# The passage from output projection to FFN with VectorE alone, on kept fp32 tiles of the first token half

## The chip, the cores and the metric

The kernel runs on one core of a Trainium2 chip, as one launch. The metric is the device time of that launch in microseconds (us). The five engines run side by side, each taking its own instructions in order: PE (TensorE, matmuls; PEld is its weight load), DVE (VectorE), ACT (ScalarE), POOL (GpSimd) and SP (SyncE, which issues most DMAs).

## The reference, cut to what matters

Two layers of a bidirectional encoder trunk over 1024 tokens of width 1024. The change lies between the end of token mixing and the start of channel mixing, so this is the part that matters:

```python
x = x + gt1 * (y @ w_out[l])                       # output projection
h = rms_norm(x, g_ffn[l]) * (1 + sc2) + sh2        # adaLN norm
f = (silu(h @ w_ffn_gate[l]) * (h @ w_ffn_up[l])) @ w_ffn_down[l]   # D_FF = 2816
x = x + gt2 * f
```

## The kernel before, in words

Activations stand transposed in SBUF: 8 channel tiles of 128 partitions by 1024 tokens, in two token halves A (first 512) and B (last 512). Every operand of a matmul is split into a rounded high part and a low part ("hi", "lo"), and each product is three matmuls (hi hi, hi lo, lo hi). ACT makes the high part, DVE or POOL subtracts it from the fp32 value for the low part.

The gate and up products of the FFN are computed by a Strassen-like scheme with seven products per block f of 128 hidden channels (22 blocks), p = 1 to 7, of 12 matmuls each. The seven data operands (`opnd`) are: operands 0 and 1, the normed half A, channel tiles 0 to 3 and 4 to 7 (called h(0..3,A), h(4..7,A)); and operands 2 to 6, sums and differences of the tiles of both halves. `prep` (L1198) makes operands 2 to 6 in five loops over k = 0 to 3:

- operand 2 = h(k,B) - h(k,A); operand 3 = h(4+k,B) - operand 2; operand 4 = h(4+k,B) - h(k,B);
- operand 5 = h(4+k,B); operand 6 = h(4+k,A) - operand 3.

`w_out` (L1157) runs the last jobs of the output projection. It first does the jobs of half A (`self.run(4)`), then weaves the norm of half A (`norm`, L389, with `h_tile`, L374, for each of 8 tiles) into the jobs of half B, and hands `prep` on as a generator. `add_x` (L1117) adds a finished projection tile to x, out of PSUM, and `square` (L345) then accumulates its square for the norm. `rstd_end` (L357) sums the squares over the partitions by 1-column matmuls and spreads the result by one more matmul.

`ffn` (L1471) starts with eight early jobs, p = 1 and 2 of the first `FIRST` = 4 blocks, which need operands 0 and 1 only; the pieces of `prep` are woven in between by the list `nb_f`. Then come p = 5, 6, 7, 3, 4 of block 0, which take operands 2, 3, 4, 5, 6 in this order, then those of block 1, and so on. The weights of a job are prepared by `load` in `p_job` (L1254): for p = 5, 6, 7, 3 a combination of raw weight tiles (`comb`, L1266), then hi on ACT and lo (L1293) on DVE or POOL. A job's weights are prepared up to three jobs ahead. The raw weights of block f + 1 are loaded by SP when the lo part of p = 4 of block f has been taken. After p = 4 of a block the hidden tile is finished on DVE and ACT (`after`, L1301; tile ffa_A), and the down product of that block follows.

The order on PE is written out by the program. For the other engines here a planner places the instructions by its own costs: an engine takes the instruction that stands earliest in the program among those that the planner holds to be ready. Which engine does an elementwise step is written in the table `TUNE` (L92): 0 is DVE, 1 is POOL. `prep`, `lo_f`, `s_f`, `sq_w` and `ht_w` are the lists that matter: the operations of `prep`; the low parts of the late jobs' weights; the weight combinations; the squares in `w_out`; and the kind of `h_tile` (kind 0 takes one scaled product on DVE, hi on ACT, lo on DVE; kind 1 takes a second ACT pass and lo on POOL).

All elementwise steps of one helper have that helper's line in the profile: L191 is a matmul, L199 an ACT step, L202 a DVE TENSOR_TENSOR, L205 a DVE SCALAR_TENSOR_TENSOR, L352 the sum of squares, L385 the lo of `h_tile` on POOL, L1211 the operations of `prep`.

Of the kernel before, what the change touches and what calls it, by code (L numbers as in the profile page):

```python
# [9 lines left out]
F32 = mybir.dt.float32  # L10
F32R = mybir.dt.float32r
AF = mybir.ActivationFunctionType
ALU = mybir.AluOpType
# [4 lines left out]
HALF = 512  # L18
# [7 lines left out]
U = 1024  # L26
# [34 lines left out]
for l in range(2):  # L61
# [8 lines left out]
               split=[38, 35, 37, 39, 41, 43, 54],  # L70
               lo=[0, 0, 0, 0, 0, 0, 0, 0, 0, 0, 0, 0, 0, 0, 0, 1, 0, 0, 0, 0, 0, 0, 0, 0, 0, 0, 0, 0, 0, 0, 0, 0, 0, 0, 0, 0, 0, 0, 0, 0, 0, 0, 0, 0, 0, 0, 0, 0, 0, 0, 0, 0, 0, 0, 0, 0, 0, 0, 0, 0, 0, 0, 0, 0, 1, 0, 0, 0, 0, 0, 0, 1],
               hi=[0, 1, 1, 1, 1, 0, 0, 0, 0, 0, 0, 1, 0, 1, 0],
# [3 lines left out]
FIRST = 4  # L76
# [6 lines left out]
               split=[35, 39, 36, 36, 43, 43, 55],  # L83
               lo=[0, 0, 0, 0, 0, 0, 0, 0, 0, 0, 0, 0, 0, 0, 0, 1, 0, 0, 0, 0, 0, 0, 0, 0, 0, 0, 0, 0, 0, 0, 0, 0, 0, 0, 1, 0, 0, 0, 0, 0, 0, 0, 0, 0, 0, 0, 0, 1, 0, 1, 0, 0, 0, 0, 1, 0, 0, 0, 0, 1, 0, 0, 0, 0, 1, 0, 0, 1, 0, 0, 0, 1],
               hi=[0, 1, 1, 1, 1, 0, 0, 0, 1, 1, 0, 1, 0, 1, 1],
# [5 lines left out]
T_BIAS[1] = 6  # L91
TUNE = dict(  # L92
    na_w=[3, 14], nb_f=[3, 8] + list(range(9, 15)) + list(range(16, 30)), na_f=[5, 11], nb_m=[3, 8],
    prep=[0, 0, 0, 0, 1, 0, 0, 1] * 2 + [0, 0, 1] * 4 + [0, 1] * 4 + [1, 0] * 2 + [0, 1, 0] * 4,
    ht_w=[0, 1] * 4, ht_a=[0, 1] * 4, ht_b=[0, 1] * 4,
    sq_w=[0, 1] * 8, sq_f=[0, 1] * 8,
    lo_e=[0] * 8, lo_f=[1, 0, 0, 1, 0] * FIRST, s_f=[1] * 4 * FIRST,
    pairs=[[2, 3, 4, 4, 5, 6, 6, 7] for _ in range(FIRST)], post=[0] * FIRST,
    fin=[[8, 15], [26, 31]], fk=[[1] * 8, [0, 1] * 4, [0, 1] * 4], sq_t=[[0, 1] * 4, [0, 1] * 4, [0] * 8],
)  # L100
# [9 lines left out]
NS = ((0, 512), (512, 512))  # L110
# [22 lines left out]
class Trunk:  # L133
# [18 lines left out]
        self.ready = set()  # L152
        self.queue, self.look, self.sq = deque(), 1, {}

# [1 line left out]
    def open(self, name, **tiles):  # L156
        cm = self.tc.tile_pool(name=name, bufs=1)
        pool = cm.__enter__()
        for nm, (n, dt) in tiles.items():
            setattr(self, nm, pool.tile([P, n], dt, name=f"{name}_{nm}"))  # L160
        return cm
# [24 lines left out]
        o = (8 * lo + k) * U + n[0]  # L186
        return self.RA[:, o:o + n[1]]

# [1 line left out]
    def mm(self, out, lhsT, rhs, start, stop):  # L190
        self.nc.tensor.matmul(out=out, lhsT=lhsT, rhs=rhs, start=start, stop=stop)  # L191

# [22 lines left out]
            self.act(hi, src, AF.Copy)  # L215
        self.tt(lo, src, hi.bitcast(F32), ALU.subtract)

# [1 line left out]
    def w_load(self, src, n, hi_eng=0):  # L219
        def go():  # L220
            raw, o = self.f(self.WR(), n), self.WH()
            self.at = o
            hi, lo = self.RA[:, o:o + n], self.RA[:, o + self.WS:o + self.WS + n]
            self.nc.sync.dma_start(out=raw, in_=src)
            self.split(raw, hi, lo, hi_eng)
            return hi, lo
        return go
# [25 lines left out]
        for _ in range(njobs):  # L253
            yield from self.pull()

# [1 line left out]
    def setup(self):  # L257
        nc = self.nc
        self.vec = self.const(2 * V_N + 8)
        self.ident = self.const(P)  # L260
        self.ones = self.const(P)
        self.mod = [self.const(48) for _ in range(DEPTH)]
        self.coef = [self.const(16) for _ in range(DEPTH)]
        self.lam8 = [self.const(12) for _ in range(DEPTH)]
        self.tiny = self.const(36)
        self.st = Ring(self.const(4) for _ in range(12))
        nc.scalar.dma_start(out=self.f(self.T0 + 3 * U, U, 0, 1), in_=self.I["c"])
        nc.scalar.dma_start(out=self.f(self.vec, 2 * V_N + 8), in_=self.I["vecs"])
        nc.scalar.dma_start(out=self.f(self.ident, P), in_=self.I["ident"])
        nc.vector.memset(self.f(self.ones, P), 1.0)  # L270
        self.epsc = self.const(1)
        self.st16 = self.const(16)
        self.nc.vector.tensor_copy(out=self.RA[:, 20 * U:20 * U + P], in_=self.f(self.ident, P))
        nc.vector.memset(self.f(self.epsc, 1), EPS)
        row = self.f(self.T0 + 3 * U, U, 0, 1)
        self.act(row, row, AF.Silu)
        for i in range(2):
            self.mm(self.bank(i), self.f(self.ones, P, 0, 1), row[:, i * HALF:(i + 1) * HALF], True, True)
# [55 lines left out]
        while self.steps is not None:  # L334
            self.bg(1)

# [1 line left out]
    def sumsq(self, n, k, acc, s, eng):  # L338
        if k == 0:
            self.act(acc, self.x(k, n), AF.Square)  # L340
# [49 lines left out]
    def norm(self, l, which, n, bank, ts, kinds):  # L390
        accs = self.sq.pop(n)[0]
        yield from self.rstd_end(n, accs, bank)
        for k in range(8):
            self.h_tile(l, which, n, k, ts[k % 2], accs[0], kinds[k])
        yield

    def h_act(self, l, which, n, k, t, twice=True):
        hi, lo = self.h(k, n, 0), self.h(k, n, 1)
# [15 lines left out]
                evac(b)  # L414
            yield

# [1 line left out]
    def jobs(self):  # L418
        for l in range(DEPTH):
            yield from self.mix_jobs(l)  # L420
# [50 lines left out]
        self.act(self.y(j, *n), b, AF.Copy)  # L471
        self.ready.add((j, n[0]))

# [1 line left out]
    def start(self):  # L475
        nc, l = self.nc, 0
        A, B = NS
# [348 lines left out]
    def k_evac(self, t, n, b):  # L826
        self.act(self.f(self.SK + n[0], n[1]), b, AF.Copy)

# [1 line left out]
    def slot_ones(self):  # L830
        for e in range(2):
            self.nc.vector.tensor_copy(out=self.slot(e, 3, 0, U, 64, 68).rearrange("p (a b) -> p a b", a=8),
# [273 lines left out]
        self.attention(l, fill)  # L1106
        return early

# [1 line left out]
    def y_split(self, j):  # L1110
        for c in (0, HALF):
            self.split(self.y(j, c, HALF), self.RA[:, j * U + c:j * U + c + HALF],
# [43 lines left out]
    def w_out(self, l):  # L1156
        A, B = NS  # L1157
        self.ps_all.i = 2
        self.y_split(7)
        self.x_load(l, 7)  # L1160
        self.c_spread()
        self.warm_sqrt(self.f(self.M0, 1))
        self.raws = Ring([self.f(self.M0 + U, U)])
        self.steps = self.mod_steps([(l, 5)] if l == 0 else [])
        self.bgn = 3
        self.hp = self.open(f"hx{l}", HX=(12 * U, F32R))
        self.pp = self.open(f"prep{l}", FP=(4 * U, F32))
        fp = lambda i: self.FP[:, i * HALF:(i + 1) * HALF]
        t = [self.f(self.T0 + HALF * i, HALF) for i in range(4)]
        self.sq[A] = [t[0], fp(7)], [fp(4), fp(5)], TUNE["sq_w"][:8]  # L1170
        self.run(4)
        na = self.norm(l, 1, A, self.ps_all(), t[2:], TUNE["ht_w"])
        self.sq[B] = [t[1], fp(6)], [fp(4), fp(5)], TUNE["sq_w"][8:]
        self.weave(3, na, TUNE["na_w"])
        self.look = 2
        o = self.WH.items[self.WH.i % 2]
        self.PR = Ring([o, o + U, 34 * U - o, 35 * U - o])
        self.weave(1, na, ())
        self.look = 3
        self.bg_all()  # L1180
        self.bgn = 0
        return self.prep(l, 0)
# [3 lines left out]
        self.nc.sync.dma_start(out=cb, in_=self.I["c"].broadcast_to((P, U)))  # L1186
        self.act(cb, cb, AF.Silu)

# [1 line left out]
    def opnd(self, j, k, lo):  # L1190
        if j in (0, 1):
            return self.h(4 * j + k, NS[0], lo)
# [3 lines left out]
        return self.HX[:, o:o + HALF]  # L1196

    def prep(self, l, bank):  # L1198
        nc, n = self.nc, NS[1]
        accs = self.sq.pop(n)[0]  # L1200
        yield from self.rstd_end(n, accs, bank)
        acc = accs[0]
        fp = lambda i: self.FP[:, i * HALF:(i + 1) * HALF]
        q1 = [fp(k) for k in range(4)]
        t = [fp(4 + k) for k in range(4)]
        q2 = [self.f(self.T0 + HALF * i, HALF) for i in (2, 3)] + \
            [self.f(10 * U + HALF * i, HALF) for i in range(2)]
        turn = iter(TUNE["prep"])

        def tt(out, a, b, op):  # L1210
            (nc.gpsimd if next(turn) else nc.vector).tensor_tensor(out=out, in0=a, in1=b, op=op)  # L1211

        def norm(q, k):
            tt(q, self.x(k, n), acc, ALU.mult)
            self.act(q, q, AF.Identity, scale=self.f(self.coef[l] + 8 + k, 1), bias=self.f(self.mod[l] + 24 + k, 1))

        def parts(j, k, src):
            hi, lo = self.opnd(j, k, 0), self.opnd(j, k, 1)
            self.act(hi, src, AF.Copy)
            tt(lo, src, hi.bitcast(F32), ALU.subtract)  # L1220

        old = lambda j, k, lo: self.opnd(j, k, lo).bitcast(F32)
        for k in range(4):
            norm(q1[k], k)
            tt(t[k], q1[k], old(0, k, 0), ALU.subtract)
            tt(t[k], t[k], old(0, k, 1), ALU.subtract)
            parts(2, k, t[k])
            yield
        for k in range(4):
            norm(q2[k], 4 + k)  # L1230
            tt(t[k], q2[k], t[k], ALU.subtract)
            parts(3, k, t[k])
            yield
        for k in range(4):
            tt(q1[k], q2[k], q1[k], ALU.subtract)
            parts(4, k, q1[k])
            yield
        for k in range(4):
            parts(5, k, q2[k])
            yield  # L1240
        for k in range(4):
            tt(t[k], old(1, k, 0), t[k], ALU.subtract)
            tt(t[k], t[k], old(1, k, 1), ALU.add)
            parts(6, k, t[k])
            yield

# [418 lines left out]
```

## Time and profile before

| | |
|---|---|
| median of 3 runs | 2447.42 us (2445.95 to 2452.44) |
| profiled execution | span 2447.3 us; the page gives no other time for it |
| busy share of the span | PE 92%, PEld 73%, DVE 78%, ACT 41%, POOL 37% |
| chain of work that ended last | PE 65%, DVE 21%, issue 5%, ACT 4%, POOL 2%, DMA 2% |
| granted TensorE clock, mean | 0.963 |

The span is one execution by the hardware profiler. The shares are means over stages of quite different kinds; the passage stands twice in the trace, once per layer, near 485 to 590 us and 1678 to 1781 us. Times are counted from the start of the span. A group "x38" is 38 instructions of one kind in a row. Bracketed behind an instruction is the time its engine sat idle before it, and what ended that.

### The profile page before, as it was taken

How to read it: one execution, taken by the hardware profiler on the slowest of the kernel's cores; microseconds unless marked ns; L12 is line 12 of the kernel's file. 1: busy time of each engine (PE TensorE's matmuls, PEld its weight loads, DVE VectorE, ACT ScalarE, POOL GpSimd, SP SyncE). 2: the span in 40 equal slices, each digit the busy share in tenths (PEclk: the TensorE clock that was granted, in tenths of full speed). 3: DMA queues.
4: the chain of work that ended last, by engine and by line, in shares of the span. 5: the costliest groups of instructions: out<-in, count | busy, mean ns of one | idle time of the engine just before them, and what ended most of it. 6: DMA issues, size and time to landing. Idle time of an engine off the chain costs nothing.

```text
span 2447.3 us, 27382 instructions
## 1 busy us (share of the span) xinstructions
PE 2252.3 (92%) x9754; PEld 1790.4 (73%) x9754; DVE 1920.1 (78%) x2732; ACT 995.3 (41%) x1638; POOL 902.7 (37%) x646
## 2 busy tenths in 40 slices
PE   6987998977999999999989899898799999999996
PEld 4765876765777777778867687677567888888885
DVE  8887789788888888887765676986987777777775
ACT  4375575453222222222354746654422222222234
POOL 4133375255233333333231316642622333333333
PEclk9998999988999999999989999999899999999998
DMA  7323422411233333331221132312111111111111
GB/s 286 104 67 116 132 96 86 148 44 65 67 110 106 110 111 109 108 104 52 78 103 51 50 103 70 120 63 87 36 65 52 52 52 52 52 52 52 52 48 69
DMA packets 77998, 206.94 MB, mean 85 GB/s; under 512 B 8995, under 2 KB 13091, under 8 KB 77862
## 3 DMA queue, kind: packets, MB, share of 16 engines
q1 hardware_dynamic: 74116, 186.55, 23.3%
q10 hardware_dynamic: 3746, 18.66, 2.2%
q8 instruction: 76, 1.25, 0.2%
q14 instruction: 60, 0.49, 0.1%
HBM read 196.79 MB, written 8.39 MB: 84 GB/s over the span
## 4 chain that ended last, share of the span: by engine, by line
PE 65%; DVE 21%; issue 5%; ACT 4%; POOL 2%; DMA 2%; SPq 0%; POOLq 0%; DVEq 0%; ACTq 0%
PE psum L191 65%; DVE plain L202 3%; DVE rounded L202 3%; DVE plain L205 2%; DVE prep_FP L1211 1%; DVE rounded L1293 1%; DMA plain<-in_ada 1%; DVE ffa_A L202 1%; DVE psum L880 1%; DVE plain L313 1%; DVE psum L202 1%; ACT lru_LF L199 1%; ACT plain L199 1%; ACT ffa_A L199 1%; ACT rounded L199 1%
## 5 line engine op out<-in xcount | busy, mean ns | idle before, releaser
L191 PE MATMUL psum<-rounded 128*128 128x512 f32 (+1 forms) x4380 | 1091.0, 398 | 73.4 <-DVE rounded L1293 21.1
L191 PEld LDWEIGHTS psum<-rounded 128*128 128x128 f32 x4380 | 834.2, 193 | 264.2 <-DVE rounded L1293 25.1
L205 DVE SCALAR_TENSOR_TENSOR plain<-psum,plain 128x1024 f32<-128x1024 f32 (+2 forms) x464 | 483.6, 1051 | 200.6 <-PE psum L191 198.4
L199 ACT ACTIVATE rounded<-plain 128x512 fp32r<-128x512 f32 (+4 forms) x464 | 307.0, 668 | 768.9 <-PE psum L191 667.4
L191 PE MATMUL psum<-ffa_A,ffa_DW 128*128 128x512 f32 (+1 forms) x2040 | 531.1, 394 | 19.1 <-ACT ffa_A L199 7.8
L191 PEld LDWEIGHTS psum<-ffa_A,ffa_DW 128*128 128x128 f32 x2040 | 378.0, 189 | 123.0 <-DVE ffa_A L202 14.9
L1266 POOL TENSOR_TENSOR plain<-plain 128x512 f32<-128x512 f32 x176 | 254.2, 1444 | 516.4 <-DMA plain<-in_wu 340.8
L191 PE MATMUL psum<-hx_HX,rounded 128*128 128x512 f32 x1584 | 408.0, 395 | 7.5 <-DVE rounded L1293 4.2
L191 PEld LDWEIGHTS psum<-hx_HX,rounded 128*128 128x128 f32 x1584 | 299.5, 189 | 77.0 <-DVE rounded L1293 5.3
L1293 POOL TENSOR_TENSOR rounded<-plain,rounded 128x512 fp32r<-128x512 f32 x124 | 175.0, 1411 | 324.1 <-ACT rounded L199 324.1
L202 DVE TENSOR_TENSOR plain<-psum,plain 128x512 f32<-128x512 f32 x316 | 211.5, 685 | 31.7 <-PE psum L191 26.2
L202 DVE TENSOR_TENSOR rounded<-plain,rounded 128x512 fp32r<-128x512 f32 (+4 forms) x139 | 150.3, 1092 | 62.1 <-ACT rounded L199 60.9
L917 POOL TENSOR_TENSOR rounded<-qk_PE,rounded 128x512 fp32r<-128x512 f32 (+3 forms) x132 | 140.9, 1074 | 127.0 <-ACT rounded L199 102.4
L199 ACT ACTIVATE plain<-plain 128x512 f32<-128x512 f32 (+4 forms) x205 | 130.5, 644 | 97.8 <-DVE plain L202 58.2
L1293 DVE TENSOR_TENSOR rounded<-plain,rounded 128x512 fp32r<-128x512 f32 x184 | 139.4, 758 | 12.6 <-ACT rounded L199 12.4
L202 DVE TENSOR_TENSOR plain<-plain 128x512 f32<-128x512 f32 (+4 forms) x162 | 142.8, 883 | 6.9 <-ACT plain L199 1.9
L191 PE MATMUL psum<-rounded,v_V 128*65 128x512 f32 (+4 forms) x528 | 128.8, 358 | 14.5 <-ACT rounded L199 4.8
L191 PE MATMUL psum<-qk_QT 128*128 128x512 f32 (+8 forms) x432 | 108.0, 349 | 21.3 <-DVE plain L880 15.3
L199 ACT ACTIVATE ffa_DW<-plain 128x512 fp32r<-128x512 f32 x84 | 53.0, 630 | 155.5 <-PE psum L191 153.9
L202 DVE TENSOR_TENSOR psum<-psum,plain 128x256 f32<-128x256 f32 x240 | 97.7, 410 | 21.0 <-PE psum L191 14.3
L191 PEld LDWEIGHTS psum<-rounded,v_V 128*65 128x65 f32 (+1 forms) x528 | 74.0, 149 | 53.0 <-POOL rounded L917 6.3
L199 ACT ACTIVATE qk_PE<-psum 128x512 f32<-128x512 f32 (+4 forms) x168 | 83.3, 503 | 55.4 <-DVE psum L202 51.3
(124 smaller groups left out, 2031.4 us busy)
## 6 DMA issues: line engine op xcount, KB each, us to landing
plain<-in_ada SPq DMA_DIRECT2D x96, 256.0 KB, 2.5
plain<-in_wg SPq DMA_DIRECT2D x44, 512.0 KB, 3.5
plain<-in_wu SPq DMA_DIRECT2D x44, 512.0 KB, 3.5
plain<-in_wd SPq DMA_DIRECT2D x88, 256.0 KB, 2.6
plain<-in_ada SPq DMA_DIRECT2D x30, 512.0 KB, 3.5
start_AT<-in_ada SPq DMA_DIRECT2D x18, 512.0 KB, 5.7
plain<-in_bias_t ACTq DMA_DIRECT2D x12, 768.0 KB, 4.8
plain<-in_bias_s ACTq DMA_DIRECT2D x12, 736.0 KB, 4.4
```

Of the source, the lines that this page charges most:

```text
L191: self.nc.tensor.matmul(out=out, lhsT=lhsT, rhs=rhs, start=start, stop=stop)
L199: self.nc.scalar.activation(out=out, in_=in_, func=func, **kw)
L202: self.nc.vector.tensor_tensor(out=out, in0=a, in1=b, op=op)
L205: self.nc.vector.scalar_tensor_tensor(out=out, in0=a, scalar=s, in1=b, op0=op0, op1=op1)
L313: self.nc.vector.tensor_tensor_reduce(out=raw, in0=raw, in1=self.f(self.M0, U), op0=ALU.mult, op1=ALU.add, scale=1.0, scalar=0.0, accum_ou ...
L880: self.nc.vector.tensor_tensor_reduce(out=s, in0=s, in1=self.f(bo, a * w).rearrange("p (a b) -> p a b", a=a), op0=ALU.add, op1=ALU.max, sc ...
L917: (self.nc.vector if PLAN[self.l]["lo"][self.step] else self.nc.gpsimd).tensor_tensor(out=pl, in0=p, in1=ph.bitcast(F32), op=ALU.subtract)
L1211: (nc.gpsimd if next(turn) else nc.vector).tensor_tensor(out=out, in0=a, in1=b, op=op)
L1266: comb = lambda out, a, b, op=ALU.subtract: (nc.gpsimd if pool_s else nc.vector).tensor_tensor(out=out, in0=a, in1=b, op=op)
L1293: (nc.gpsimd if pool_lo else nc.vector).tensor_tensor(out=lo, in0=src, in1=hi.bitcast(F32), op=ALU.subtract)
```

## The change

- `TUNE["prep"]` goes; every operation of `prep` is on DVE. In `sq_w`, `ht_w`, `s_f` of block 0 and `lo_f` of block 0 all ones become zeros: squares in `w_out`, lo parts of the A tiles, the four combinations and two lo parts of block 0 go from POOL to DVE.
- The eight scaled A tiles (x times scale times 1/rms, before the shift) stay in fp32 in the upper half of the tile FP, which grows from 4U to 8U columns; `h_tile` no longer alternates two temporaries.
- `prep` works on scaled tiles without shift. In operand 2 the shift cancels. In operands 3, 5 and 6 it enters as the scalar of a SCALAR_TENSOR_TENSOR, in operand 4 as the difference of two shifts (`ds`, one small instruction). The two subtractions of the hi and lo parts of half A become one with the kept tile; the ACT pass that applied scale and shift goes.
- `dynamic_dma_scratch_size=512` is passed when the program is built, which leaves more SBUF for tiles.

```diff
-    prep=[0, 0, 0, 0, 1, 0, 0, 1] * 2 + [0, 0, 1] * 4 + [0, 1] * 4 + [1, 0] * 2 + [0, 1, 0] * 4,
-    ht_w=[0, 1] * 4, ht_a=[0, 1] * 4, ht_b=[0, 1] * 4,
-    sq_w=[0, 1] * 8, sq_f=[0, 1] * 8,
-    lo_e=[0] * 8, lo_f=[1, 0, 0, 1, 0] * FIRST, s_f=[1] * 4 * FIRST,
+    ht_w=[0] * 8, ht_a=[0, 1] * 4, ht_b=[0, 1] * 4,
+    sq_w=[0] * 16, sq_f=[0, 1] * 8,
+    lo_e=[0] * 8, lo_f=[0] * 5 + [1, 0, 0, 1, 0] * (FIRST - 1), s_f=[0] * 4 + [1] * 4 * (FIRST - 1),
...
-            self.h_tile(l, which, n, k, ts[k % 2], accs[0], kinds[k])
+            self.h_tile(l, which, n, k, ts[k % len(ts)], accs[0], kinds[k])
...
+    def kept(self, k):
+        return self.FP[:, (8 + k) * HALF:(9 + k) * HALF]
...
-        self.pp = self.open(f"prep{l}", FP=(4 * U, F32))
+        self.pp = self.open(f"prep{l}", FP=(8 * U, F32))
...
-        na = self.norm(l, 1, A, self.ps_all(), t[2:], TUNE["ht_w"])
+        na = self.norm(l, 1, A, self.ps_all(), [self.kept(k) for k in range(8)], TUNE["ht_w"])
...
-        def norm(q, k):
-            tt(q, self.x(k, n), acc, ALU.mult)
-            self.act(q, q, AF.Identity, scale=self.f(self.coef[l] + 8 + k, 1), bias=self.f(self.mod[l] + 24 + k, 1))
+        ds = self.f(self.st16, 4)
+        self.tt(ds, self.f(self.mod[l] + 28, 4), self.f(self.mod[l] + 24, 4), ALU.subtract)
+
+        def scaled(q, k):
+            self.stt(q, self.x(k, n), sc(k), acc, ALU.mult, ALU.mult)
...
         for k in range(4):
-            norm(q1[k], k)
-            tt(t[k], q1[k], old(0, k, 0), ALU.subtract)
-            tt(t[k], t[k], old(0, k, 1), ALU.subtract)
+            scaled(q1[k], k)
+            self.tt(t[k], q1[k], self.kept(k), ALU.subtract)
             parts(2, k, t[k])
             yield
         for k in range(4):
-            norm(q2[k], 4 + k)
-            tt(t[k], q2[k], t[k], ALU.subtract)
+            scaled(q2[k], 4 + k)
+            self.stt(t[k], q2[k], sh(4 + k), t[k], ALU.add, ALU.subtract)
             parts(3, k, t[k])
             yield
         for k in range(4):
-            tt(q1[k], q2[k], q1[k], ALU.subtract)
+            self.stt(q1[k], q2[k], ds[:, k:k + 1], q1[k], ALU.add, ALU.subtract)
             parts(4, k, q1[k])
             yield
         for k in range(4):
-            parts(5, k, q2[k])
+            hi, lo = self.opnd(5, k, 0), self.opnd(5, k, 1)
+            self.act(hi, q2[k], AF.Identity, bias=sh(4 + k))
+            self.stt(lo, q2[k], sh(4 + k), hi.bitcast(F32), ALU.add, ALU.subtract)
             yield
         for k in range(4):
-            tt(t[k], old(1, k, 0), t[k], ALU.subtract)
-            tt(t[k], t[k], old(1, k, 1), ALU.add)
+            self.stt(t[k], self.kept(4 + k), sh(4 + k), t[k], ALU.add, ALU.subtract)
             parts(6, k, t[k])
             yield
...
-    nc = _bacc.Bacc("TRN2", target_bir_lowering=False, num_devices=1)
+    nc = _bacc.Bacc("TRN2", target_bir_lowering=False, num_devices=1, dynamic_dma_scratch_size=512)
```

## Rows read from the trace of the kernel before

**Rows 1.** Busy time by stretch: window; its length, then busy us (count) per engine, PEclk.
```profile
500.00:525.96 25.96, 20.04 (x84) 15.72 (x83) 21.62 (x27) 14.62 (x25) 12.70 (x8) 0.87 0.14 47
525.96:571.70 45.74, 29.00 (x101) 21.71 (x100) 45.74 (x39) 22.75 (x37) 35.63 (x22) 0.81 0.08 29
571.70:588.20 16.50, 11.62 (x47) 8.16 (x46) 13.79 (x18) 8.34 (x13) 9.82 (x7) 1.00 0.28 83
1692.70:1718.74 26.04, 19.97 (x83) 15.97 (x82) 17.66 (x25) 13.82 (x22) 10.69 (x7) 0.87 0.13 48
1718.74:1764.50 45.76, 29.25 (x98) 21.62 (x97) 45.76 (x39) 22.76 (x37) 35.65 (x22) 0.80 0.07 23
1764.50:1781.15 16.65, 12.96 (x50) 9.40 (x48) 13.95 (x18) 8.43 (x13) 9.83 (x7) 0.91 0.27 81
```

**Rows 2.** Timeline of PE, first layer: start, us, engine, line, operation [idle before <-releaser].
```profile
498.45 9.42 PE L191 MATMUL psum<-rounded 128*128 128x512 f32 x39
512.75 5.11 PE L191 MATMUL psum<-rounded 128*128 128x512 f32 x12 [4.89 <-ACT rounded L199]
...
545.66 4.64 PE L191 MATMUL psum<-rounded 128*128 128x512 f32 x10 [4.33 <-DVE rounded L1293]
...
562.62 4.63 PE L191 MATMUL psum<-rounded 128*128 128x512 f32 x10 [4.77 <-DVE rounded L1293]
...
575.13 2.92 PE L191 MATMUL psum<-rounded 128*128 128x512 f32 x12
...
579.70 2.57 PE L191 MATMUL psum<-hx_HX,rounded 128*128 128x512 f32 x10 [1.18 <-POOL rounded L1293]
...
588.20 1.84 PE L191 MATMUL psum<-ffa_A,ffa_DW 128*128 128x512 f32 x5 [1.72 <-DVE ffa_A L202]
```

**Rows 3.** Timeline of DVE, first layer.
```profile
501.05 1.77 DVE L205 SCALAR_TENSOR_TENSOR plain<-plain 128x512 f32<-128x512 f32 x1
...
503.92 0.74 DVE L205 SCALAR_TENSOR_TENSOR plain<-plain 128x512 f32<-128x512 f32 x1
504.58 0.73 DVE L205 SCALAR_TENSOR_TENSOR plain<-psum,plain 128x512 f32<-128x512 f32 x1
505.24 1.12 DVE L205 SCALAR_TENSOR_TENSOR rounded<-plain,rounded 128x512 fp32r<-128x512 f32 x1
...
529.97 4.79 DVE L1211 TENSOR_TENSOR prep_FP<-prep_FP,rounded 128x512 f32<-128x512 f32 x6
...
571.04 0.68 DVE L1293 TENSOR_TENSOR rounded<-plain,rounded 128x512 fp32r<-128x512 f32 x1
571.64 0.68 DVE L202 TENSOR_TENSOR plain<-psum,plain 128x512 f32<-128x512 f32 x1
573.58 0.69 DVE L1211 TENSOR_TENSOR rounded<-prep_FP,rounded 128x512 fp32r<-128x512 f32 x1 [1.26 <-ACT rounded L199]
```

**Rows 4.** Timeline of POOL, first layer.
```profile
532.60 1.61 POOL L1211 TENSOR_TENSOR hx_HX<-prep_FP,hx_HX 128x512 fp32r<-128x512 f32 x1 [3.10 <-ACT hx_HX L199]
...
575.39 3.02 POOL L1266 TENSOR_TENSOR plain<-plain 128x512 f32<-128x512 f32 x2 [2.51 <-DMA plain<-in_wu]
578.38 1.27 POOL L1293 TENSOR_TENSOR rounded<-plain,rounded 128x512 fp32r<-128x512 f32 x1
```

**Rows 5.** Timeline of PE, second layer.
```profile
1690.91 9.42 PE L191 MATMUL psum<-rounded 128*128 128x512 f32 x39
1706.40 5.46 PE L191 MATMUL psum<-rounded 128*128 128x512 f32 x12 [6.07 <-DVE plain L205]
...
1769.52 2.93 PE L191 MATMUL psum<-rounded 128*128 128x512 f32 x12
...
1781.15 2.50 PE L191 MATMUL psum<-ffa_A,ffa_DW 128*128 128x512 f32 x5 [1.72 <-DVE ffa_A L202]
```

**Rows 6.** DMA queues of the page: queue, kind, packets, MB, share.
```profile
q10 hardware_dynamic: 3746, 18.66, 2.2%
q8 instruction: 76, 1.25, 0.2%
```

More of the change, by code (lines that the diff above doesn't have):

```diff
@@ L1198, in prep @@
     def prep(self, l, bank):
-        nc, n = self.nc, NS[1]
+        n = NS[1]
         accs = self.sq.pop(n)[0]
@@ L1207, in prep @@
             [self.f(10 * U + HALF * i, HALF) for i in range(2)]
-        turn = iter(TUNE["prep"])
-        def tt(out, a, b, op):
-            (nc.gpsimd if next(turn) else nc.vector).tensor_tensor(out=out, in0=a, in1=b, op=op)
-        def norm(q, k):
-            tt(q, self.x(k, n), acc, ALU.mult)
-            self.act(q, q, AF.Identity, scale=self.f(self.coef[l] + 8 + k, 1), bias=self.f(self.mod[l] + 24 + k, 1))
+        sc = lambda k: self.f(self.coef[l] + 8 + k, 1)
+        sh = lambda k: self.f(self.mod[l] + 24 + k, 1)
+        ds = self.f(self.st16, 4)
+        self.tt(ds, self.f(self.mod[l] + 28, 4), self.f(self.mod[l] + 24, 4), ALU.subtract)
+        def scaled(q, k):
+            self.stt(q, self.x(k, n), sc(k), acc, ALU.mult, ALU.mult)
         def parts(j, k, src):
@@ L1219, in parts @@
             self.act(hi, src, AF.Copy)
-            tt(lo, src, hi.bitcast(F32), ALU.subtract)
-        old = lambda j, k, lo: self.opnd(j, k, lo).bitcast(F32)
+            self.tt(lo, src, hi.bitcast(F32), ALU.subtract)
         for k in range(4):
-            norm(q1[k], k)
-            tt(t[k], q1[k], old(0, k, 0), ALU.subtract)
-            tt(t[k], t[k], old(0, k, 1), ALU.subtract)
+            scaled(q1[k], k)
+            self.tt(t[k], q1[k], self.kept(k), ALU.subtract)
             parts(2, k, t[k])
```

## The prediction, on record before the changed kernel ran

> **What bounds the kernel now.** I read the page first: PE is busy nearly throughout, but its row of slices dips twice, at the passage of each layer. Then I cut the two passages into stretches [rows 1]. From 525.96 to 571.70 us DVE is busy for all of 45.74 us while PE runs only 101 matmuls; the second layer repeats this to 0.02 us. Then the timelines of PE and DVE show who ends PE's idle time: mostly the low parts of weights (L1293) or an `add_x` (L205) queued on DVE [rows 2, 3, 5]. So between the start of `prep` and the last weight of block 0 the passage is as long as DVE's queue.
>
> DVE's steps have two lengths there. Where POOL is idle, a TENSOR_TENSOR starts 0.60 us after the one before (571.04, 571.64) and a SCALAR_TENSOR_TENSOR 0.66 us after it (503.92, 504.58, 505.24) [rows 3]. Of the six from 529.97, which take 4.79 us, five at 0.60 leave one of about 1.7: POOL was idle for 3.10 us before its instruction at 532.60 [rows 4]. The 38 steps from 525.96 to 571.64 take 45.7 us, 1.20 each; at 0.60 they would take 22.8. The excess is 22.9 us, and POOL ran 22 instructions in that stretch [rows 1]: each costs DVE 1.04 us.
>
> The Trainium skill (SBUF — State Buffer, "Who interferes with whom") says that of a VectorE instruction with two SBUF inputs and a GpSimd instruction that reads SBUF, the one that comes second blocks until the first is through. By it a POOL instruction would cost DVE its whole length, 1.27 us when alone [rows 4], and the stretch would be 22.8 + 22 x 1.27 = 50.7 us; the trace has 45.7, so the block is a little less than whole. Its bearing here is on the chance of the third rival only, which it lowers.
>
> **The change, part by part.** The sum goes against the profiled execution: the page gives its span, 2447.3 us, and nothing around it; the median of the runs lies 0.1 us above.
>
> *Prep stretch.* Before, DVE did 34 of `prep`'s 52 operations per layer and POOL 18, by the list. After, DVE does 44: scaled 8, shift forms 4 + 4 + 4 + 4 (loops 2 to 5) make 24 SCALAR_TENSOR_TENSOR, and 20 TENSOR_TENSOR are left. At the unblocked steps [rows 3]: 24 x 0.66 + 20 x 0.60 = 27.8 us. The low parts of seven weights stand in the same stretch (two of block 3's early jobs, five of block 0; two of these were POOL's): 7 x 0.60 = 4.2. Of the four combinations of block 0, two need only raw weights and can go into gaps ahead of `prep`; two wait for the buffer of another and stay: 1.2. `ds` is bounded by 0 and one step, 0.6; I take 0.6. One pause for ACT's high part, as the 1.26 at 573.58 [rows 3]. Sum 35.1 us against 45.7: 10.6 us less per layer. Bounds: all four combinations inside and three pauses, 38.8 us; none and no pause, 32.0.
>
> ACT loses 8 passes of `prep` and 4 of `h_tile`; it was busy 22.75 of 45.74 us [rows 1], so this counts nothing, and there is room if a high part comes late.
>
> *Norm of half A.* Four low parts of tiles (0.66 each) and two or three squares (0.60) move to DVE, 2.6 + 1.5 = 4.1 us, against eight POOL instructions that blocked it in 25.96 us [rows 1]. With eight buffers nothing holds the 16 tile steps back, and they stand in the program ahead of the last two `add_x`. The last `add_x` frees the PSUM bank of the first early job: PE ended its 39 projection matmuls at 507.87 and restarted at 512.75; in the second layer 1700.33 and 1706.40 [rows 2, 5]. If the planner keeps program order, 16 x 0.66 = 10.6 us from the first tile step at 501.05 [rows 3], two weights and two `add_x` (2.5) give 514, 1.3 us later than now; counted from 1692.7, 1705.8, 0.6 earlier. If it serves `add_x` as soon as its matmuls end, PE restarts 4.1 and 5.4 us earlier. I take nothing, as nearest the first; both ends go into the range.
>
> *Behind the stretch.* After the last weight PE had 6.3 us until p = 4 ended (571.70 to 578.05) and 7.95 in the second layer [rows 1, 2, 5], since jobs had piled up. After, PE is the follower: two jobs of 2.92 us [rows 2] from about 0.8 us before the last weight, 5.0 us. That gives 1.3 and 2.9 us more. From the end of p = 4 to the first down product 10.15 us pass, 8.7 in the second layer [rows 2, 5]: block 1's weights are still on POOL and DVE finishes the hidden tile, so this I leave. What is late next is block 1's p = 5: its raw weights are loaded by SP only after the last weight of block 0, then two combinations and a low part on POOL; 571.70 to 579.70, 8.0 us [rows 2, 4]. That is 3.0 us after p = 4 in the new order, and its 18 matmuls (4.4 us) then end before the first down product can start. So it costs nothing while the 10 us stay; without them it would hold the gain at 10.6.
>
> *The rest.* Early squares of half A on DVE: one 0.60 step in place of a POOL step ahead of the norm's matmuls; 1.27 - 0.60 = 0.7 us either way [rows 3, 4], taken as 0. The larger FP is opened where attention's tiles ended long before and closed as before: 0. The scratch size: the page's four queues are two of each kind [rows 6], none that POOL feeds, so 0; a longer landing time of SP's loads would show otherwise.
>
> Sum: layer one 10.6 + 1.3 = 11.9, layer two 10.6 + 2.9 = 13.5, together 25.4. PE is near full after each passage, so the shift carries to the end. 2447.3 - 25.4 = 2421.9, against the median **2422 us**. Own range 2414 to 2430.
>
> **Rivals.**
> 1. *The norm stage shortens too.* The planner serves the last `add_x` in time: 4.1 + 5.4 = 9.5 us more, 2412. With the shorter pause the first early job may run at the upper clock level (2.92 instead of 5.1 us for 12 matmuls [rows 2]; it now runs at half rate after 4.89 us idle): 4.4 more, 2408. I set 2410. For it: POOL's locks fill the norm stretch. Against: sixteen tile steps ahead in the program.
> 2. *Block 0's weights queue behind all of `prep`.* Its low parts stand late in the program. Then PE gets p = 5 after 27.8 + 0.6 + 1.2 + 1.3 + 0.6 = 31.5 us, the first job at half rate 5.1, four at 2.9: 48.2 us from the start of `prep` to the end of p = 4, against 52.1 and 53.7: 9.4 us in all, **2438**. For it: L1293 is what PE waits for already at 545.66 and 562.62 [rows 2].
> 3. *The long steps are not POOL's doing but the passage's* (PE, ACT and DMA reading SBUF at the same time). Then 53 DVE steps at 1.20 us take 63.8 us against 45.7: +36 in all, **2484**, slower. It decides at 45.7 / 53 = 0.86 us per step. For it: DVE is already busy for the whole stretch, and the change gives it work. Against: the 0.60 steps of the same kind of instruction with POOL idle. The Trainium skill (Perfetto Trace Analysis, "Optimizing Scalar/DVE Operations") says that work of a saturated DVE may be offloaded to Scalar or even GPSIMD, the reverse of this change; by it one would end on this side. The same paragraph adds that between those two the shared port may leave no gain, and the two step lengths here bear that out.
> 4. *No change.* What is gained is given back: the planner orders the rest of the program otherwise, or block 1 waits for its loads and its hidden tile 10 us longer. About 2446. Against: POOL's and DVE's work behind 571.70 is untouched.
>
> **How the numbers follow.** Forecast 0.46, first rival 0.22, second 0.20, fourth 0.07, third 0.05. About 0.3% (7 us) is what a measurement here can tell from no change. Forecast and first two rivals are faster: 0.88; same 0.07; slower 0.05. The range leaves out the third and fourth and the outer edges of the rest: 2405 to 2439.
>
> **What would show it.** Right: in the prep stretch POOL near 0 instructions, DVE full with steps of 0.60 to 0.66, the stretch 32 to 39 us long; the first early job near 513 and 1706; p = 4 of block 0 ends about 12 us earlier, the first down product too. Wrong: many DVE steps over 1 us without POOL (third); the first early job near 509 (first); PE waiting on L1293 for p = 5 to 4 with the operands long done (second); or a prep stretch that is shorter while the first down product hasn't moved (fourth).

## The result, and the profile after

The changed kernel takes 2417.43 us (median of 4 runs, 2413.6 to 2419.18) against 2448.8 us before (4 runs): ratio 0.9867, 95% interval 0.9851 to 0.9882, 31.4 us faster. The forecast was 2422, its range 2405 to 2439. A second series beside other kernels gave 2415.94 against 2448.58, ratio 0.9864 (0.985 to 0.9877). The profiled execution has a span of 2411.8 us and took 2413.6 us in all, so 1.8 us lie around the span; it is the fastest of its series.

The busy time by stretch of the changed kernel, cut at the same events as [rows 1] (columns as there: window; length, busy us and count of PE, PEld, DVE, ACT and POOL, then PEclk, the granted TensorE clock as a share of full speed, the DMA share and GB/s). Helpers stand one line earlier in this kernel: L190 is a matmul, L198 an ACT step, L201 a TENSOR_TENSOR, L204 a SCALAR_TENSOR_TENSOR; the operations of `prep` now go through the last two.

```profile
500.00:524.96 24.96, 16.45 (x72) 13.09 (x71) 18.74 (x31) 10.54 (x17) 0.00 (x0) 0.86 0.13 42
524.96:558.41 33.45, 27.71 (x105) 20.27 (x103) 33.45 (x54) 18.79 (x31) 0.00 (x0) 0.90 0.10 28
558.41:571.69 13.28, 10.58 (x41) 7.31 (x41) 11.85 (x16) 7.05 (x12) 7.55 (x5) 1.00 0.23 88
...
1701.25:1734.71 33.46, 26.86 (x105) 19.85 (x103) 33.46 (x54) 18.66 (x31) 0.00 (x0) 0.95 0.08 21
1734.71:1747.89 13.18, 11.36 (x41) 8.62 (x41) 11.81 (x15) 7.08 (x12) 7.59 (x5) 0.87 0.22 89
```

POOL does nothing up to the last weight of block 0. DVE now does 54 steps in 33.45 us, 0.62 each, where it did 39 in 45.74. PE is still not full there (27.71 us): DVE's queue sets the length as before, it is only shorter.

The timeline of PE in the first layer of the changed kernel, to be held against [rows 2] (of block 0's jobs p = 5, 7 and 3 read operands in hx_HX, p = 6 and 4 in `rounded`):

```profile
495.60 9.42 PE L190 MATMUL psum<-rounded 128*128 128x512 f32 x39
513.53 4.67 PE L190 MATMUL psum<-rounded 128*128 128x512 f32 x12 [8.51 <-DVE plain L204]
...
538.96 2.58 PE L190 MATMUL psum<-rounded 128*128 128x512 f32 x10 [1.28 <-DVE rounded L1293]
541.37 0.62 PE L190 MATMUL psum<-hx_HX,rounded 128*128 128x512 f32 x2
545.88 4.63 PE L190 MATMUL psum<-hx_HX,rounded 128*128 128x512 f32 x10 [3.89 <-DVE rounded L1293]
...
560.89 2.91 PE L190 MATMUL psum<-rounded 128*128 128x512 f32 x12
...
566.30 2.58 PE L190 MATMUL psum<-hx_HX,rounded 128*128 128x512 f32 x10 [1.65 <-POOL rounded L1293]
...
571.69 1.44 PE L190 MATMUL psum<-ffa_A,ffa_DW 128*128 128x512 f32 x5 [0.86 <-DVE ffa_A L201]
```

The reader is to see three things: the first early job now waits longer for the last `add_x` (8.51 us, 4.89 before); the waits ahead of p = 5 to 4 have nearly gone but for one of 3.89; the first down product comes at 571.69, 16.5 us earlier. [rows 2] and the prediction take that product from its second matmul, the one that waited for DVE, and so does this text; its first matmul starts at 570.43, against 585.98 before. And the second layer, against [rows 5]:

```profile
1673.39 9.42 PE L190 MATMUL psum<-rounded 128*128 128x512 f32 x39
1688.75 5.46 PE L190 MATMUL psum<-rounded 128*128 128x512 f32 x12 [5.95 <-DVE plain L204]
...
1737.17 2.91 PE L190 MATMUL psum<-rounded 128*128 128x512 f32 x12
...
1747.89 1.54 PE L190 MATMUL psum<-ffa_A,ffa_DW 128*128 128x512 f32 x6
```

The order on PE is the same in both kernels, so each matmul's start can be matched. The lead of the changed kernel, in us:

| at | layer 1 | layer 2 |
|---|---|---|
| start of the last 39 projection matmuls | 2.85 | 17.5 |
| start of `prep` on DVE | 1.0 | 17.5 |
| last weight of block 0 | 13.3 | 29.8 |
| end of p = 4 | 14.25 | 32.4 |
| first down product (second matmul) | 16.5 | 33.0 |
| some 50 us on | 17.6 | 35.4 |

So the passages give 17.6 - 2.85 = 14.75 and 35.4 - 17.5 = 17.9 us, 32.6 in all. The 2.85 us of lead ahead of the first passage are not the change's: a second profile of the same kernel has 0.0 there, and 14.9 and 17.9 us in the passages. The medians of the two series differ by 31.4 and 32.6 us.

### The profile page after: what moved, and what is told of

It is laid out like the page before. It is cut to its first block, busy times and chain, and to the rows that moved or that the text cites. A ratio compares the mean times of both kernels' runs of the same rounds, so it can differ in the third digit from the quotient of the medians.

```text
span 2411.8 us, 27313 instructions
## 1 busy us (share of the span) xinstructions
PE 2244.1 (93%) x9754; PEld 1784.6 (74%) x9754; DVE 1899.5 (79%) x2786; ACT 978.8 (41%) x1614; POOL 791.8 (33%) x578
## 4 chain that ended last, share of the span: by engine, by line
PE 63%; DVE 23%; issue 5%; ACT 3%; DMA 3%; POOL 2%; POOLq 0%; SPq 0%; DVEq 0%; ACTq 0%
PE psum L190 63%; DVE rounded L201 3%; DVE plain L204 3%; DVE plain L201 3%; DMA plain<-in_ada 2%; DVE prep_FP L204 1%; DVE ffa_A L201 1%; DVE rounded L1293 1%; DVE plain L312 1%; DVE psum L882 1%; ACT plain L198 1%; DVE plain L1434 1%; DVE psum L201 1%; ACT lru_LF L198 1%; ACT ffa_A L198 1%
## 5 line engine op out<-in xcount | busy, mean ns | idle before, releaser
L190 PE MATMUL psum<-rounded 128*128 128x512 f32 (+1 forms) x4380 | 1079.6, 395 | 50.4 <-DVE plain L204 15.3
L190 PEld LDWEIGHTS psum<-rounded 128*128 128x128 f32 x4380 | 828.2, 192 | 236.7 <-issue 21.7
L204 DVE SCALAR_TENSOR_TENSOR plain<-psum,plain 128x1024 f32<-128x1024 f32 (+2 forms) x464 | 483.5, 1051 | 195.3 <-PE psum L190 193.2
L198 ACT ACTIVATE rounded<-plain 128x512 fp32r<-128x512 f32 (+4 forms) x448 | 296.2, 666 | 760.6 <-PE psum L190 675.9
L190 PE MATMUL psum<-ffa_A,ffa_DW 128*128 128x512 f32 (+1 forms) x2040 | 528.8, 392 | 12.7 <-ACT ffa_A L198 5.5
L1266 POOL TENSOR_TENSOR plain<-plain 128x512 f32<-128x512 f32 x168 | 240.4, 1431 | 725.7 <-DMA plain<-in_wu 428.4
L190 PEld LDWEIGHTS psum<-ffa_A,ffa_DW 128*128 128x128 f32 x2040 | 376.4, 188 | 116.2 <-DVE plain L204 13.4
L190 PE MATMUL psum<-hx_HX,rounded 128*128 128x512 f32 x1584 | 412.1, 397 | 14.5 <-DVE rounded L1293 8.6
L190 PEld LDWEIGHTS psum<-hx_HX,rounded 128*128 128x128 f32 x1584 | 300.0, 190 | 86.8 <-DVE rounded L1293 11.4
L1293 POOL TENSOR_TENSOR rounded<-plain,rounded 128x512 fp32r<-128x512 f32 x120 | 168.2, 1401 | 319.7 <-ACT rounded L198 319.7
L201 DVE TENSOR_TENSOR plain<-psum,plain 128x512 f32<-128x512 f32 x316 | 211.6, 685 | 30.3 <-PE psum L190 24.6
L201 DVE TENSOR_TENSOR rounded<-plain,rounded 128x512 fp32r<-128x512 f32 (+4 forms) x139 | 147.9, 1075 | 59.5 <-ACT rounded L198 58.3
L198 ACT ACTIVATE plain<-plain 128x512 f32<-128x512 f32 (+5 forms) x189 | 118.2, 634 | 100.4 <-DVE plain L201 68.1
L201 DVE TENSOR_TENSOR plain<-plain 128x512 f32<-128x512 f32 (+6 forms) x164 | 145.4, 888 | 7.2 <-ACT plain L198 2.3
L1293 DVE TENSOR_TENSOR rounded<-plain,rounded 128x512 fp32r<-128x512 f32 x188 | 137.4, 732 | 15.7 <-ACT rounded L198 15.2
L190 PE MATMUL psum<-rounded,v_V 128*65 128x512 f32 (+4 forms) x528 | 130.0, 361 | 14.0 <-ACT rounded L198 4.0
L190 PE MATMUL psum<-qk_QT 128*128 128x512 f32 (+8 forms) x432 | 107.9, 349 | 19.4 <-DVE plain L882 13.3
L198 ACT ACTIVATE ffa_DW<-plain 128x512 fp32r<-128x512 f32 x84 | 53.0, 630 | 151.7 <-PE psum L190 150.6
L201 DVE TENSOR_TENSOR psum<-psum,plain 128x256 f32<-128x256 f32 x240 | 97.8, 410 | 21.1 <-PE psum L190 14.4
L190 PEld LDWEIGHTS psum<-rounded,v_V 128*65 128x65 f32 (+1 forms) x528 | 75.0, 151 | 52.5 <-POOL rounded L919 6.4
L198 ACT ACTIVATE qk_PE<-psum 128x512 f32<-128x512 f32 (+4 forms) x168 | 83.3, 503 | 55.7 <-DVE psum L201 49.7
```

The costliest lines, as they stand in the source:

```text
L198: self.nc.scalar.activation(out=out, in_=in_, func=func, **kw)
L201: self.nc.vector.tensor_tensor(out=out, in0=a, in1=b, op=op)
L204: self.nc.vector.scalar_tensor_tensor(out=out, in0=a, scalar=s, in1=b, op0=op0, op1=op1)
L1266: comb = lambda out, a, b, op=ALU.subtract: (nc.gpsimd if pool_s else nc.vector).tensor_tensor(out=out, in0=a, in1=b, op=op)
L1293: (nc.gpsimd if pool_lo else nc.vector).tensor_tensor(out=lo, in0=src, in1=hi.bitcast(F32), op=ALU.subtract)
```

## The experiments

**Idle work on POOL.** The changed kernel with twelve subtractions added on POOL; the added line stands behind `parts` in loops 1 to 3 (shown for loop 1; loops 2 and 3 take their own tiles).

```diff
+            self.nc.gpsimd.tensor_tensor(out=self.opnd(5, k, 1), in0=q1[k], in1=t[k], op=ALU.subtract)
```

> The changed kernel with 12 more POOL subtractions per layer in loops 1 to 3 of the preparation, whose results are overwritten and which nothing waits for but the buffers' next writers. Theory (each POOL instruction blocks DVE by 1.04 us): the prep stretch grows from 33.4 to about 45.9 us in each layer, with DVE steps near 1.7 us again, and the kernel is about 25 us slower than the changed one (18 to 28): 2442. Rival (long DVE steps come from the passage's other traffic, not from POOL): DVE steps stay at 0.60 to 0.66 us, the time within 4 us of the changed kernel.

Measured 2442.32 us (2438.62 to 2445.51), ratio to before 0.9965 (0.9953 to 0.9978): 26 us slower than the changed kernel's 2415.94 (2417.43 in the first series). The two prep stretches, and four groups of DVE's timeline in the first:

```profile
525.01:571.07 46.06, 28.79 (x105) 21.13 (x103) 46.06 (x54) 18.81 (x31) 20.13 (x12) 0.81 0.08 21
1715.41:1761.43 46.02, 30.11 (x105) 22.50 (x103) 46.02 (x54) 18.80 (x31) 20.09 (x12) 0.78 0.05 14
```

```profile
531.56 0.68 DVE L201 TENSOR_TENSOR prep_FP<-prep_FP 128x512 f32<-128x512 f32 x1
532.16 0.74 DVE L204 SCALAR_TENSOR_TENSOR prep_FP<-plain 128x512 f32<-128x512 f32 x1
532.82 1.78 DVE L1296 TENSOR_TENSOR rounded<-plain,rounded 128x512 fp32r<-128x512 f32 x1
534.52 0.68 DVE L201 TENSOR_TENSOR hx_HX<-prep_FP,hx_HX 128x512 fp32r<-128x512 f32 x1
```

The same 54 DVE steps take 12.6 us more, 1.05 per POOL instruction, though nobody reads what POOL computes. The next writers of its tiles could have to wait for it, but DVE is busy for the whole stretch: the time is in its steps. DVE has the two lengths of step of the kernel before again, and each POOL instruction lengthens one step: in the first layer 12 of the 54 take 1.75 us or more, the others at most 0.74. In the kernel before it was 21 of 39 beside 22 POOL instructions, in the changed kernel none. The third rival has fallen.

**The rewriting without the engines.** The changed kernel, with 14 of the 16 low parts that `parts` makes in the preparation, and block 0's weights (four combinations, two low parts), back on POOL.

```diff
+        turn = iter([0, 1, 0, 1] + [1] * 8 + [1] * 4)
...
-            self.tt(lo, src, hi.bitcast(F32), ALU.subtract)
+            (self.nc.gpsimd if next(turn) else self.nc.vector).tensor_tensor(
+                out=lo, in0=src, in1=hi.bitcast(F32), op=ALU.subtract)
...
+    lo_f=[1, 0, 0, 1, 0] * FIRST, s_f=[1] * 4 * FIRST,
```

> The rewritten preparation, but 14 of its 20 TENSOR_TENSOR low parts per layer and the weights of block 0 go back to POOL; the norm of half A stays on DVE. Theory (the gain is POOL's block of DVE): DVE keeps 30 operations of the preparation and five weight low parts in the prep stretch, about 22 us, and some 18 POOL instructions cost it 1.04 us each, 18.7: 40.8 us against 33.4 in the changed kernel and 45.7 before; so about 15 us slower than the changed kernel, near 2432. Rival (the gain is the smaller number of operations and POOL's share runs free beside DVE): the stretch is 22 to 25 us and the kernel some 15 to 20 us faster than the changed one, near 2400.

Measured 2439.95 us (2438.31 to 2444.93), ratio to before 0.996 (0.9947 to 0.9972). The stretches of this kernel:

```profile
532.86:573.23 40.37, 28.06 (x102) 21.78 (x101) 40.37 (x36) 18.05 (x30) 29.86 (x18) 0.84 0.10 33
1721.39:1761.80 40.41, 28.96 (x108) 22.39 (x107) 40.41 (x36) 18.05 (x30) 29.91 (x18) 0.83 0.09 27
```

36 DVE steps take longer than the changed kernel's 54: 40.4 us, where 40.8 was expected. The kernel is 2440 where 2432 was expected: it lost more than the stretch gives (2 x 6.9 us). Block 0's weights alone cost 11.0 us outside the stretch, below, which is about the rest.

**The engines without the rewriting.** The kernel before, with its lists set to DVE (`prep=[0] * 52`, and `sq_w`, `ht_w`, `lo_f`, `s_f` as in the change).

> The kernel before with its 52 operations of the preparation, its squares, tile low parts and block 0's weights all on DVE, nothing rewritten. Theory (POOL's block): prep stretch 52 x 0.60 + 4.2 + 1.2 = 36.6 us against 33.4 in the changed kernel, so 3.2 us more per layer, about 6 us slower than the changed kernel: 2424 (2419 to 2430). Rival (the rewriting brings the gain): the stretch stays at 45 us or grows, and the time stays at 2440 or above.

Measured 2421.68 us (2421.33 to 2431.43), ratio to before 0.9892 (0.9874 to 0.9909). Its stretches:

```profile
524.69:560.91 36.22, 28.23 (x105) 20.47 (x103) 36.22 (x61) 22.96 (x38) 0.00 (x0) 0.91 0.10 26
1708.51:1744.88 36.37, 28.62 (x105) 21.33 (x103) 36.31 (x61) 22.86 (x38) 0.00 (x0) 0.86 0.06 18
```

36.3 us against 33.45: the eight operations fewer are worth 2.8 us per layer, the engines 9.4. By the ratios (0.9892 against 0.9867) about four fifths of the gain are the table's and one fifth is the rewriting's, but the two intervals overlap. ACT did as much here as before (22.96 us in the stretch, 22.75 before), so less work for ACT isn't what brings the gain.

**Block 0's weights back on POOL.** The changed kernel with `lo_f=[1, 0, 0, 1, 0] * FIRST, s_f=[1] * 4 * FIRST`.

> The changed kernel with the four combinations and two low parts of block 0's weights back on POOL. Theory: inside the prep stretch two combinations and two low parts, 4 x (1.04 - 0.60) = 1.8 us more per layer, and a little in the norm stage: 3 to 6 us slower than the changed kernel, 2421. Rival (so few instructions find gaps of DVE, which costs nothing, or are worth their parallel run): within 2 us, or faster.

Measured 2429.24 us (2428.99 to 2434.27), ratio 0.9924 (0.9911 to 0.9936): 13.3 us slower than the changed kernel beside it, more than twice what was expected. The stretch itself grew by 1.2 us, near the 1.8 expected. The other two terms were missed. DVE in the norm stage of this kernel:

```profile
503.32 2.44 DVE L204 SCALAR_TENSOR_TENSOR rounded<-prep_FP,plain,rounded 128x512 fp32r<-128x512 f32 x2
505.68 1.77 DVE L204 SCALAR_TENSOR_TENSOR prep_FP<-plain 128x512 f32<-128x512 f32 x1
```

Two early combinations on POOL block two tile steps, and the last `add_x` stands behind them. PE behind the stretch, and two rows of DVE:

```profile
563.05 6.90 PE L190 MATMUL psum<-hx_HX,rounded 128*128 128x512 f32 x22 [2.50 <-DVE rounded L1293]
569.79 2.93 PE L190 MATMUL psum<-rounded 128*128 128x512 f32 x12
...
580.81 2.50 PE L190 MATMUL psum<-ffa_A,ffa_DW 128*128 128x512 f32 x5 [1.73 <-DVE ffa_A L201]
```

```profile
574.65 0.69 DVE L1293 TENSOR_TENSOR rounded<-plain,rounded 128x512 fp32r<-128x512 f32 x1 [0.15 <-ACT rounded L198]
575.26 0.68 DVE L201 TENSOR_TENSOR plain<-psum,plain 128x512 f32<-128x512 f32 x1
```

With the weights on POOL the planner puts the low part for p = 7 only just ahead of that for p = 4 (564.27, its end), PE needs 8.5 us from there to the end of p = 4 (5.4 in the changed kernel), and the first down product comes 16.5 us after the last weight, as in the kernel before (571.72 to 588.20 [rows 2, 3]). In the changed kernel it is 13.3. By layer: ahead of `prep` 2.9 and 1.0, in the stretch 1.2 and 1.1, behind it up to the first down product 3.3 and 3.2, and 1.0 and 2.2 in the 50 us after that; together 15.9 us in the two passages. The medians differ by 13.3; what gives the rest back outside the passages was not traced.

**Norm of half A back on POOL.** The changed kernel with `ht_w=[0, 1] * 4, sq_w=[0, 1] * 8`; kind 1 shifts a copy of the kept tile.

> The changed kernel with half A's norm stage as before: every second square and every second tile's low part on POOL (from a copy that ACT shifts), the preparation still on DVE and on kept tiles. Theory (POOL blocks DVE there too, but what PE waits for is the place of the last add_x): eight POOL instructions at 1.04 us against 4.1 us of DVE steps saved, so DVE loses about 4 us per layer, of which part is hidden: 0 to 8 us slower than the changed kernel, 2420. Rival (in this stage DVE is the bound by its own steps, and POOL's help is worth more than its block): the first early job starts 2 to 4 us earlier in each layer and the kernel is 3 to 8 us faster, 2412.

Measured 2417.41 us (2411.58 to 2419.62), ratio 0.9865 (0.9848 to 0.9882): no difference from 0.9864. The first early job waits much as in the changed kernel (8.51 us there):

```profile
518.50 4.31 PE L190 MATMUL psum<-rounded 128*128 128x512 f32 x12 [9.13 <-DVE plain L204]
```

Moving the norm's steps from POOL to DVE is worth nothing by itself, as the prediction had it. The eight kept tiles stay in this run, so it doesn't tell what they do to the order.

**Four tiles later.** The changed kernel, with `h_tile` 4 to 7 put behind the last `add_x` in the program.

```diff
             self.h_tile(l, which, n, k, ts[k % len(ts)], accs[0], kinds[k])
+            if which and k == 3:
+                yield
...
-        self.weave(1, na, ())
+        self.weave(1, na, (7,))
```

> The changed kernel, with the second four of half A's eight normed tiles put into the program behind the last add_x of the output projection. Theory (in the norm stage PE waits for the last add_x, which stands behind 16 tile steps on DVE): the first early job starts near 506 and 1684 instead of 513.5 and 1688.8, runs at the upper clock level, and the preparation starts 5 to 8 us earlier in each layer: 10 to 16 us faster than the changed kernel, near 2404. Rival (the tiles themselves are what is late): the first early job starts earlier, but the second then waits for its tiles, the preparation starts when it did, and the time is within 3 us of the changed kernel.

Measured 2404.6 us (2400.37 to 2405.06), ratio to before 0.9808 (0.9795 to 0.9821): faster than both kernels. PE in this kernel, first and second layer:

```profile
498.77 9.42 PE L190 MATMUL psum<-rounded 128*128 128x512 f32 x39
511.39 4.42 PE L190 MATMUL psum<-rounded 128*128 128x512 f32 x12 [3.21 <-DVE plain L204]
...
1674.08 9.42 PE L190 MATMUL psum<-rounded 128*128 128x512 f32 x39
1684.79 3.02 PE L190 MATMUL psum<-rounded 128*128 128x512 f32 x12 [1.30 <-ACT rounded L198]
```

From the start of the 39 projection matmuls to the start of `prep` (522.54 and 1694.57) it takes 23.8 and 20.5 us, against 29.4 and 27.9 in the changed kernel: 5.6 and 7.4 us less, 13.0 in all, and the median moved by 11 to 13. The twelve matmuls behind PE's wait take 3.02 us after 1.30 us idle (granted clock 1.00), 4.42 after 3.21 (0.65), and 5.46 after 5.95 in the changed kernel's second layer (0.50): the upper level was reached in the second layer only.

**Block 1's weights on DVE too**, on top of the last one (`lo_f=[0] * 10 + ...`, `s_f=[0] * 8 + ...`).

> The version with the second four tiles behind the last add_x, and block 1's weight combinations and low parts on DVE as well. Theory (POOL still blocks DVE between the last weight of block 0 and the first down product, five instructions at about 1.04 against 0.60): about 2 us faster per layer than that version, 2400. Rival (DVE has no room there, since it finishes the hidden tile at the same time): no gain or 1 to 3 us slower, 2405 to 2408.

Measured 2403.43 us (2402.51 to 2403.76), ratio 0.9812 (0.9799 to 0.9825), as without it (0.9808). In its profile the two passages are 1.2 and 1.8 us shorter than without it, near the 2 us per layer of the theory, but the medians are only 1.2 us apart and one range lies within the other. The times show neither the 4 us nor a loss, and what POOL's block costs behind the last weight stays open.

**Weights ahead of loop 3.** The weaving list of the changed kernel:

```diff
-    nb_f=[3, 8] + list(range(9, 15)) + list(range(16, 30)),
+    nb_f=[3, 8] + list(range(9, 15)) + [16, 20] + list(range(20, 32)),
```

> The changed kernel with the pieces of the preparation's loops 3 to 5 woven in later, so that the weights of block 0's p = 5 and p = 6 stand ahead of loop 3 and the end of loop 4 in the program. PE's wait of 3.9 us ahead of p = 5 should shrink. Theory (DVE's queue up to the last weight of block 0 sets the end of the passage, and the order inside it does not): prep stretch stays at 33.5 us, the first down product stays, time within 4 us of the changed kernel, 2416. Rival (PE's wait for the weights of p = 5 is itself what is lost): 6 to 8 us faster, 2409.

Measured 2421.37 us (2415.39 to 2422.49), ratio 0.9878 (0.9862 to 0.9895), which overlaps the changed kernel's interval. The prep stretch is 33.46 us in both layers, as before the move. The wait ahead of p = 5 is gone, and a longer one stands ahead of p = 6:

```profile
545.71 2.92 PE L190 MATMUL psum<-hx_HX,rounded 128*128 128x512 f32 x12
553.39 5.90 PE L190 MATMUL psum<-rounded 128*128 128x512 f32 x12 [4.77 <-ACT rounded L198]
```

Within the stretch PE's visible waits are where DVE's queue happens to be felt. The same weaving on the version with four tiles later:

> The same weaving on the version with the second four tiles behind the last add_x. Theory: within 4 us of that version, 2404. Rival: 6 to 8 us faster, 2397.

2405.55 us (2400.7 to 2406.43), ratio 0.9817 (0.9803 to 0.983): no change either.

**The scratch size alone**, on the kernel before.

> The kernel before with the smaller DMA scratch alone. Theory (no queue uses it): within 0.3% of the kernel before, 2448. Rival (the lead of 3 us that the changed kernel's first profile has already ahead of the first passage comes from it): 3 us faster throughout the opening, 2445.

2451.68 us (2447.74 to 2455.32), ratio 1.0008 (0.9999 to 1.0017): nothing.

The last run, listed for completeness, was the changed kernel again:

> The changed kernel once more, as the measure for the three others beside it: 2417 (2413 to 2420).

## Why the prediction was right, step by step

- *What bounds the passage, and the price of POOL.* Right. 1.04 us per POOL instruction was read from the kernel before; twelve idle ones cost 1.05 each. The rows for the short steps were not all read where POOL is idle, as the prediction says: while DVE ran those at 503.92 to 505.24, POOL was at work,

```profile
502.23 3.58 POOL L1266 TENSOR_TENSOR plain<-plain 128x512 f32<-128x512 f32 x2
```

  and it began another step at 571.20. That these steps are short was luck: about one step is lengthened per POOL instruction, and it was not these. The 0.60 and 0.66 hold, as the 54 steps of the changed kernel beside an idle POOL show, none of them over 0.75 us long.
- *Prep stretch.* 35.1 us were forecast, 33.45 measured, in both layers. The steps (27.8 + 4.2 + 1.2 = 33.2) were right; the pause for ACT (1.3) did not come, and `ds` is not in the stretch but far ahead of it (446.22 in the first layer). 1.6 us per layer too little gain. Two combinations went ahead of `prep`, as supposed.
- *Norm of half A.* Taken as 0, with 1.3 us later and 0.6 earlier as the end for program order: the first early job came 3.6 us later relative to the projection in the first layer, 0.1 earlier in the second; the start of `prep` 1.85 later and 0. The mechanism, tile steps ahead of the last `add_x`, is shown by the version that moves four of them; that it is the eight buffers which let all of them go ahead was not tried. In the first layer its size was above the bound.
- *Behind the stretch.* The end of p = 4 was put 5.0 us after the last weight; it is 5.4. The 10.15 and 8.7 us from there to the first down product were left as they were: a term that was mis-sized. They are 7.9 and 8.0. In the kernel before, the sum that needs p = 4 (at 582.66) stood on DVE behind the low part of a later weight, which waited for POOL and ACT; after, it comes as soon as the product ends (578.05 and 563.80). The rows of DVE before, and then after:

```profile
582.05 0.69 DVE L1293 TENSOR_TENSOR rounded<-plain,rounded 128x512 fp32r<-128x512 f32 x1 [0.15 <-ACT rounded L199]
582.66 0.68 DVE L202 TENSOR_TENSOR plain<-psum,plain 128x512 f32<-128x512 f32 x1
```

```profile
563.83 0.69 DVE L201 TENSOR_TENSOR plain<-psum,plain 128x512 f32<-128x512 f32 x1 [1.02 <-PE psum L190]
564.44 0.68 DVE L201 TENSOR_TENSOR plain<-plain 128x512 f32<-128x512 f32 x1
```

  From the last weight to the first down product it is 16.5 and 16.6 us before, 13.3 and 13.4 after, and 16.5 and 16.7 with block 0's weights on POOL, where the sum stands behind that low part again (575.26, the end of p = 4 being 572.7). So the 3.2 us per layer go with block 0's weights on DVE. How they split at the end of p = 4 does not: with the weights on POOL it is 8.1 and 8.3 us from there, nearly as in the changed kernel, and the loss lies ahead of it. Why the planner orders so was not tried.
- *The rest.* Right behind the first down product the lead grows by 1.1 and 2.3 us more and then stays, which the prediction had at nothing ("the shift carries to the end"). It is PE's rate: the same matmuls run slower in the kernel before. The six behind the product's first six take 2.74 us at 589.84, and 1.52 at 572.97 in the changed kernel. The granted clock (the number behind POOL's) of the stretches from the first down product on, before and after:

```profile
588.20:600.00 11.80, 11.80 (x42) 8.74 (x43) 8.25 (x12) 1.90 (x3) 5.14 (x4) 0.86 0.18 64
1781.15:1800.00 18.85, 18.68 (x66) 13.97 (x67) 13.55 (x20) 2.53 (x4) 6.39 (x5) 0.84 0.17 57
```

```profile
571.69:583.00 11.31, 11.00 (x44) 7.96 (x45) 10.70 (x15) 1.96 (x4) 5.99 (x5) 1.00 0.39 118
1747.89:1765.00 17.11, 16.74 (x69) 12.17 (x68) 15.88 (x24) 2.68 (x5) 8.29 (x6) 1.00 0.33 98
```

  Ahead of 588.20 PE had been idle for 1.99 and 1.72 us with one matmul between them; ahead of 571.69 only for 0.86. With block 0's weights on POOL this gain, too, is gone (0.1 us in each layer).
- *Sum.* 25.4 forecast, 31.4 measured by the medians, 32.6 by the passages of the profiles. The terms close on the latter: 25.4 and 3.3 from the stretch, 2.9 from the down product's wait and 3.4 from the clock behind it, less 0.7 for the end of p = 4 and 1.9 in the norm stage, give 32.4. So the forecast is near because the path was right, and partly because the terms that it missed go both ways.
- *Rivals.* The first was wrong for the change, but its place was right: 11 to 13 us were to be had there by moving the tiles, where it had 9.5 and, with the clock, 13.9. The second didn't come: the low parts of block 0's weights stand among the steps of `prep`, and the passages shrank by more than its 9.4 us. Nor did the fourth: the first down product moved with the stretch. The Trainium skill (SBUF — State Buffer, "Who interferes with whom") has the second of the two instructions wait until the first is through; by that, as an estimate, the twelve idle POOL instructions, 1.27 us when alone [rows 4], would cost 15.2 us. The trace has 12.6, so the block is real and not quite whole.

## What to carry to other kernels

Where an engine has steps of two lengths for one form of instruction, look at what its neighbour does at these moments before counting the neighbour's help as free: here a subtraction on POOL cost DVE 1.05 us, and DVE does it itself in 0.60. In a stretch that one in-order queue bounds, count that queue's steps and not PE's waits; moving a wait about inside the stretch left its end where it was. When temporaries become plentiful, steps that used to be held back may crowd ahead of the one that another engine waits for, so look again at what stands in front of it.

## What the runs showed of the hardware that was not expected

Both sides of the block pay: among DVE's steps POOL's instruction of 1.27 us takes 1.68 on average (20.13 us for 12), and one step of DVE's for each, 0.68 or 0.74 otherwise, takes 1.74 to 1.79. So one POOL subtraction beside a full DVE queue costs more DVE time than the same subtraction on DVE.
